# Padded operand tiles and rearranged joints in a two-block fp32 transformer kernel

## The chip, the cores and the metric

The kernel runs on one core of a Trainium2 chip. The metric is the device time of one launch in microseconds (us): before the change the median of three runs is 3501.79 us (3500.44 to 3502.34). The engines are named as in the profile: PE is TensorE (the matmuls), PEld its weight loads, DVE is VectorE, ACT is ScalarE, POOL is GpSimd, SP is the engine that issues most DMAs. SBUF is the on-chip memory, PSUM the accumulators of PE.

## The reference

256 tokens of width 2048 go through two blocks, all in fp32.

Block 1 normalises x, projects it by `w_in`, and feeds an RWKV-7 recurrence and a sparse causal attention; `w_mix_out` joins them. A cross-attention over 256 memory rows follows (`w_q_cross`, `w_kv_cross`, `w_o_cross`), then an MLP, `square(relu(rms_norm(h) @ w_up)) @ w_down` with 8192 hidden columns, and a final norm.

Block 2 puts 16 meta tokens in front, projects by `w_in_2`, runs 8 stick-breaking heads and 8 forgetting heads, joins them by `w_out_2`, and ends in an expert layer:

```
q = h @ w_query;  s = q . sub_keys;  top 16 of each half, top 16 of their sums
idx, g = the 16 experts of each of 8 heads, softmax of their scores
a = gelu(u[idx] . h);   out = sum over h,k of (g * a) * v[idx]
```

There are 16384 experts with a row of 2048 in `u` and one in `v`.

## The kernel before

**The matmuls.** Tokens lie along the free dimension: a tile holds 128 features on the partitions and 256 tokens beside each other. A product of 2048 features is 16 such tiles. Every fp32 operand is split into a high part and a low part of a shorter format (`xh`, `xl` for tokens; `whi`, `wlo` for weights), and each block of 128x128 weights takes three matmuls, high by high, high by low, low by high, which add up in one PSUM tile `plin`. A column of 128 outputs over 2048 features is 48 matmuls. The token operand is the one that streams through PE (the moving operand, 256 columns); the 128x128 weights are loaded first.

**The weights.** `half` (L285) loads 512 KB of weights, eight 128x128 blocks, into one of four `raw` buffers through SP's queue. ACT copies each 128x512 quarter of it to `whi`, DVE subtracts to get `wlo`. `linear` (L305) walks the columns and asks for a half whenever eight blocks are used up; each finished column goes to an `evac` function, by which DVE (and ACT, POOL) take it out of PSUM.

**The norms.** A norm's factor per token needs a sum of squares over all features: POOL or ACT square and add, `colsum` sums over partitions by four small matmuls (`pcs`), DVE takes an inverse square root in a chain of small operations on 128x2 elements (`rsv`, `rsh`, `rst`, `ldr`), and `bcast` spreads it over the partitions by matmuls (`pbc`). The factor is applied after the projection. For x, `load_norm` (L425) calls `inv_rms` (L458) right after the loads. In the cross-attention's output, `out` (L1219) adds a column to `h`, splits it and has POOL square and add it (`sqt`, `acc`), column by column; its first four columns are computed together, in four PSUM tiles.

**The expert layer.** All of `u` is multiplied (`pu`, 256 halves, tokens `ph`/`pl` moving), so that `A` holds gelu(u . h) for all 16384 experts and 256 tokens; `et` is the product times the norm's factor, on its way to `A`. The chosen g are scattered by indirect DMAs (`gd`) into a table in DRAM, which is zero elsewhere. `experts_out` (L1753) then takes the experts in 128 groups j: it loads the group's g (128x256, behind a dependency on the complete table), POOL multiplies it by `A`, ACT and DVE split it into `wh` and `wl`, and two halves of `pv` are multiplied with it into eight PSUM tiles `o`. Here the roles are changed: `wh` and `wl` are the loaded 128x128 operand, and the weights `whi` and `wlo` are the moving one, 512 columns at a time.

**Order and places.** The order on each engine is worked out when the program is built, from the order of the code, from a simulation of durations, and from marks: `high_priority` lifts what is in it forward, `keep_in_program_order` (in `half`: `pin`) holds a DMA at its place among the other pinned ones. Tiles of a pool are laid out one behind the other in the order in which they are first asked for, at multiples of 32 bytes within each partition. So a tile that is asked for and never used moves those behind it.

Of the kernel before, what the change touches and what calls it, by code (L numbers as in the profile page):

```python
# [8 lines left out]
F32 = mybir.dt.float32  # L9
# [3 lines left out]
AF = mybir.ActivationFunctionType  # L13
OP = mybir.AluOpType
# [3 lines left out]
S = 256  # L18
D = 2048
KT = D // 128  # L20
NMETA = 16
# [100 lines left out]
NCOL_IN = len(W_COLS)  # L122
# [61 lines left out]
def _layout(inp):  # L184
    a = {k: np.asarray(v) for k, v in inp.items()}
    o = {}
    o["x"] = _tT(a["x"][0])
    o["mem"] = _tT(a["mem"][0])
    o["pos"] = np.ascontiguousarray(a["positions"].reshape(1, S))
    o["vecs"] = _vecs(a)  # L190
    cc = _const_arrays()
    o["ident"] = np.ascontiguousarray(cc["ident"])
    o["iota"] = np.ascontiguousarray(cc["iota"])
    o["consts_a"] = np.ascontiguousarray(np.concatenate([cc[n] for n in CA], 1))
    o["dups"] = np.ascontiguousarray(np.concatenate([cc["dup"], cc["rdup"]], 1)[:64])
# [12 lines left out]
    fl = np.concatenate([w2[:, 7168:], w2[:, 7168:], np.zeros((D, 112), w2.dtype)], 1)  # L208
    qkv = w2[:, :6144].reshape(D, 2, 3, 8, 128).transpose(0, 1, 3, 2, 4).reshape(D, 6144)
    o["w_in2"] = _blocks(np.concatenate([qkv[:, :3072], fl, qkv[:, 3072:], w2[:, 6144:7168]], 1))  # L210
    o["w_out2"] = _blocks(a["w_out_2"][0])
    o["w_pq"] = _blocks(a["peer_w_query_2"][0])
    o["keys"] = np.ascontiguousarray(a["peer_sub_keys_2"][0].reshape(16, NKEY, 128).transpose(2, 0, 1))
    u = a["peer_u_2"][0].reshape(NKEY, NKEY, KT, 128)
    o["pu"] = np.ascontiguousarray(
        u.transpose(1, 3, 2, 0).reshape(NKEY, 128, 2, 8, 128).transpose(0, 2, 1, 3, 4)).reshape(2 * NKEY, 128, 8, 128)
    v = a["peer_v_2"][0].reshape(NKEY, NKEY, 2, 1024)
    o["pv"] = np.ascontiguousarray(v.transpose(1, 2, 0, 3)).reshape(2 * NKEY, 128, 8, 128)
    return o
# [25 lines left out]
class Kernel:  # L245
# [180 lines left out]
    def load_norm(self, src, gain, xh, xl, dst, eps, acc, w, tiles):  # L426

        nc = self.nc
        ts = []
        for q in range(4):  # L430
            t = tiles(q)
            with self.tc.high_priority():
                self.tc.keep_in_program_order(nc.sync.dma_start(t, src[:, 4 * q:4 * q + 4]))
            ts.append(t)
            if q < 2:
                self.ahead.append(self.half(w[len(self.ahead)], True))
            for k in range(4):
                self.split(xh[:, 4 * q + k], xl[:, 4 * q + k], t[:, k], self.v(gain, 4 * q + k))
            if q:
                self.squares(ts[q - 1], acc, q == 1, q == 1)  # L440
        with self.tc.high_priority():
            self.tc.keep_in_program_order(nc.sync.dma_start(self.ident, self.io["ident"]))
        self.squares(ts[3], acc, False)
        self.inv_rms(dst, acc, eps)

    def squares(self, t, acc, first, pool=False):

# [9 lines left out]

    def inv_rms(self, dst, acc, eps):  # L458
        r = self.small("ldr")
        with self.tc.high_priority():  # L460
            p = self.colsum([acc[:, 0], acc[:, 1]], S)
            self.rsqrt(r, p[:, 0:2], 1.0 / D, eps)
            self.bcast(dst, r, S)

    def block1(self, c0):
        nc, tc = self.nc, self.tc
# [4 lines left out]
        xp = self.pool("xa", 1, xstack)  # L471
        yp = self.pool("yp", 1, xstack)
        ctx = ExitStack()
        cp = self.pool("ca", 1, ctx)
        ph = self.pool("pa", 1, ctx)
        ca = cp.tile([128, wid], F32, name="ca")
        C = {n: ca[:, o:o + w] for n, (o, w) in off.items()}
        self.C = C
        xh = xp.tile([128, KT, S], F32R, name="xh", tag="xh")
        xl = xp.tile([128, KT, S], F32R, name="xl", tag="xl")  # L480
        rx = ph.tile([128, S], F32, name="rx")
# [63 lines left out]

        def evac(c, p):
            kind, g, q = KIND[c]
            if kind == "dsa":
                self.dsa_evac(g, p)
            elif kind == "rwkv":  # L550
                w, j = divmod(q, 2)
# [6 lines left out]
                shift(c, p, cur["AR"][:, j, 1] if w == 0 else cur["KV"[w - 1]][:, j])  # L558
                if q == 5:
                    rs.append(self.rwkv_group(g, cur["AR"], cur["K"], cur["V"], fr))  # L560
            elif g == 0:
                self.first = shift(c, p, L)
                self.act(th, L[0:64], AF.Tanh)
                ds.append(loads())
                ds.append(low_rank())
                ds.append(self.tables())
            elif g == 1:
                shift(c, p, M)
                self.act(sM[64:96], M[64:96], AF.Sigmoid)
                ds.append(self.dsa_ki())  # L570
            else:
                shift(c, p, XG)
                self.act(XG, XG, AF.Sigmoid)
# [8 lines left out]
        self.ds = (ds, ds2)  # L582

        def dense():
            yield from self.linear(self.io["w_in"], 0, NCOL_IN, KT, xh, xl, S, evac, more=(2,))
            rm = ph.tile([128, S], F32, name="rm")
            kv = self.kv = kvp.tile([128, 8, S], F32, name="kv", tag="kv")

# [16 lines left out]
                    self.squares(tile(c), xacc, c == 0)  # L605

            yield from self.linear(self.io["w_kvc"], 0, 8, KT, xh, xl, S, kv_evac)
            self.inv_rms(rm, xacc, 1e-5)
            for c in range(8):
                self.gtt(kv[:, c], kv[:, c], rm, OP.mult)  # L610

# [506 lines left out]
            self.gtt(acc, acc, t, OP.add)  # L1118

    def rstd(self, acc, dst, eps, dim=D):  # L1120
        p = self.colsum([acc], S)
        r = self.small("rr")
        self.rsqrt(r, p[:, 0:2], 1.0 / dim, eps)
        self.bcast(dst, r, S)
        return r
# [39 lines left out]
    def cross(self, cp, cxh, cxl, rc):  # L1165
# [48 lines left out]

        self.drive(self.linear(self.io["w_qc"], 0, 4, KT, cxh, cxl, S, query), todo, 1, flush=False)
        self.mxh, self.mxl = self.pair(self.xb)
        acc = wk.tile([128, S], F32, name="acc2", tag="acc", bufs=2)

        def out(c, p):  # L1219
            self.vtt(h[:, c], p, h[:, c], OP.add)  # L1220
            self.norm_tile(c, h[:, c], "norm_mlp", self.mxh[:, c, 0:S], self.mxl[:, c, 0:S], acc, wk)


        first = [self.plin.tile([128, 512], F32, name="plin", tag="plin") for _ in range(2)] + [self.ps("pc"), self.ps("pc")]
# [23 lines left out]
            out(c, first[c][:, 0:S])  # L1248
        self.lin(self.io["w_oc"], 2, KT - 4, 4, oh, ol, S, out, c0=4)
        self.rm = wk.tile([128, S], F32, name="rmlp", tag="rc", bufs=2)  # L1250
        self.rstd(acc, self.rm, 1e-5)

    def mlp(self, up):
        nc, h, wk = self.nc, self.h, self.wk
        U = {}
        g12 = wk.tile([128, KT], F32, name="g12")
        o1, o2 = self.vec["norm_final"][0], self.vec["norm_mix_2"][0]
        self.vtt(g12, self.vecs[:, o1:o1 + KT], self.vecs[:, o2:o2 + KT], OP.mult)
# [51 lines left out]
            if g < 3:  # L1310
                up_cols(g + 1, 1, 15)

        p1, p2 = self.colsum([acc1], S), self.colsum([acc2], S)
        r1, m, r2 = self.small("r1"), self.small("m2"), self.small("r2")
        self.rsqrt(r1, p1[:, 0:2], 1.0 / D, 1e-5)
        self.vtt(m, r1, r1, OP.mult)
        self.vtt(m, m, p2[:, 0:2], OP.mult)
        self.rsqrt(r2, m, 1.0 / D, 1e-6)
        self.vtt(r2, r2, r1, OP.mult)
        self.bcast(self.r12[:, NMETA:], r2, S)  # L1320
        r1b = wk.tile([128, S], F32, name="r1b", tag="rc", bufs=2)
        self.bcast(r1b, r1, S)
        for c in range(KT):
            self.gtt(h[:, c], h[:, c], r1b, OP.mult)

    def meta_tokens(self):

# [20 lines left out]
    def block2(self):  # L1348
# [8 lines left out]
        nc.sync.dma_start(ca, self.io["consts_b"])  # L1357
        C = self.C = {n: ca[:, o:o + w] for n, (o, w) in off.items()}
        bxh, bxl, r12 = self.bxh, self.bxl, self.r12
        rs = wk.tile([128, S], F32, name="r12s", tag="rc", bufs=2)  # L1360
        self.ts(rs, r12[:, NMETA:], 128 ** -0.5, None, OP.mult)
        gq = self.small("gq", 1)
        self.ts(gq, self.v("fox_q_gain_2", 0), 128 ** -0.5, None, OP.mult)

# [3 lines left out]
        yh, yl = self.pair(self.pool("xxb", 1, mx, side="right"))  # L1368
        acc_sb = wk.tile([128, S], F32, name="accsb", tag="acc", bufs=2)
        acc_fo = wk.tile([128, S], F32, name="accfo", tag="acc", bufs=2)  # L1370
        s0, s1 = [], []
        NB = [(0, 128), (128, 128), (256, 16)]
        X16 = b2.tile([16, SP], F32, name="X16")
        B16 = b2.tile([16, SP], F32, name="B16")
# [154 lines left out]
        def evac(c, p):  # L1529
            if c == 24:  # L1530
                forget(p)
            elif c < 49:
                hd, w = divmod(c - (c > 24), 3)
                nn, n0 = ((S, NMETA), (SP, 0), (SP, 0))[w]
                t = cur[w] = b2.tile([128, nn], F32, name="qkv"[w] + "_", tag="qkv"[w], bufs=3)
                self.vtt(t, p, rs if c < 24 and w == 0 else r12[:, n0:], OP.mult)
                if w == 2:
                    st = (s0, s1)[hd % 2]
                    st.append((stick if hd < 8 else fox)(hd % 8, cur[0], cur[1], t))
# [21 lines left out]
            self.vtt(h[:, c], p, h[:, c], OP.add)  # L1561
            self.norm_tile(c, h[:, c], "norm_ffn_2", self.pxh[:, c, 0:S], self.pxl[:, c, 0:S], acc, wk)

        self.lin(self.io["w_out2"], 0, KT, KT, yh, yl, S, out)
        self.rf = self.xa.tile([128, S], F32, name="rf")
        self.rstd(acc, self.rf, 1e-6)
        mx.close()
# [192 lines left out]
    def experts_out(self, es):  # L1760
        nc, A, sp = self.nc, self.A, self.sp
        with ExitStack() as c:
# [12 lines left out]
            for j in range(NKEY):  # L1775
                w = A[j // 32][:, j % 32]
                with self.tc.high_priority():
# [4 lines left out]
                        self.tc.add_manual_dep(i.ins, x.ins.name, order if prev else sync, reason="the table is complete")  # L1782
                    prev = i
                    self.gtt(g, w, g, OP.mult)
                    wh, wl = ((sp if j == 0 else vp).tile([128, S], F32R, name=n) for n in ("wh", "wl"))
                    self.split(wh, wl, g)
                for hf in range(2):
                    hi, lo = self.half(self.io["pv"][2 * j + hf])
                    first, last = j == 0, j == NKEY - 1
                    for d in range(2):  # L1790
                        for b in range(2):
# [31 lines left out]
```

## Time and profile before

| | |
|---|---|
| median of 3 runs | 3501.79 us (3500.44 to 3502.34) |
| the profiled execution | 3498.64 us |
| its span, first to last instruction | 3496.9 us |
| PE busy | 3451.6 us, 99% of the span |
| PEld, DVE, ACT, POOL busy | 93%, 66%, 50%, 25% |
| mean granted clock of PE | 0.996 |

The span is 1.7 us shorter than the profiled execution's own time. Matmuls overlap: one lasts some 0.28 us from its start to its modelled end, and the next starts 0.12 us after it. What a matmul costs is therefore read from starts, or from the number of matmuls in a stretch in which PE is always busy, and not from the mean duration in a group. A granted clock of 1.00 is PE's higher level (2.4 GHz), 0.50 its lower one (1.2 GHz).

### The profile page before, as it was taken

The page shows a single profiled execution, that of the slowest core. Times are in us where ns is not written, and L with a number is a line of the kernel's source. Part 1 is how long each engine was busy: PE and PEld are TensorE (multiplying, and loading weights), DVE is VectorE, ACT ScalarE, POOL GpSimd, SP SyncE. Part 2 cuts the span into 40 slices and gives each one's busy share as a digit, 9 for nine tenths or more (in the row PEclk, how much of TensorE's full clock was granted, in tenths as well). Part 3 has the DMA queues.
Part 4 walks back from the last instruction along what each step waited for, and adds up shares of the span by engine and source line. Part 5 has one row for each costly group of instructions (what it writes and reads, how often), then busy time and mean ns, then how long its engine had stood idle before and what let it go on. Part 6 is the DMA issues. An engine that isn't in the chain of part 4 may idle for free.

```text
span 3496.9 us, 72405 instructions
## 1 busy us (share of the span) xinstructions
PE 3451.6 (99%) x28376; PEld 3240.5 (93%) x28376; DVE 2298.9 (66%) x4248; ACT 1762.9 (50%) x3187; POOL 880.1 (25%) x788
## 2 busy tenths in 40 slices
PE   8999999999999999999999999999999999999999
PEld 7899889899999999999999999999999888888887
DVE  7678767765656568656557799755555566666666
ACT  5444555554545455444445455555555455555554
POOL 2222213310101015200003002777777011111111
PEclk9999999999999999999999999999999999999999
DMA  5333435476767575544345656777777666666666
GB/s 198 113 119 128 165 124 184 148 218 192 226 190 228 185 230 183 158 145 145 121 133 176 202 180 188 185 186 186 187 187 185 206 210 213 211 213 211 210 214 194
DMA packets 230279, 635.99 MB, mean 182 GB/s; under 512 B 58320, under 2 KB 75408, under 8 KB 229552
## 3 DMA queue, kind: packets, MB, share of 16 engines
q1 hardware_dynamic: 193072, 631.22, 57.5%
q0 software_dynamic: 36864, 0.15, 2.3%
q8 instruction: 222, 3.64, 0.4%
q14 instruction: 121, 0.99, 0.1%
HBM read 610.16 MB, written 21.10 MB: 181 GB/s over the span
## 4 chain that ended last, share of the span: by engine, by line
PE 96%; DVE 2%; DMA 1%; issue 1%; ACT 0%; POOL 0%; DVEq 0%; SPq 0%; ACTq 0%; POOLq 0%
PE plin L255 68%; PE o L255 21%; PE po L255 1%; DVE wlo L261 1%; PE pfz L255 1%; PE pw L255 0%; PE pbc L255 0%; DMA hd<-ht 0%; PE pz L255 0%; PE pix L255 0%; PE pcs L255 0%; PE px L751 0%; PE pt L751 0%; DVE xl L264 0%; PE py L255 0%
## 5 line engine op out<-in xcount | busy, mean ns | idle before, releaser
L261 DVE TENSOR_TENSOR wlo<-raw,whi 128x512 fp32r<-128x512 f32 x2208 | 1602.7, 728 | 959.2 <-ACT whi L276 857.9
L276 ACT ACTIVATE whi<-raw 128x512 fp32r<-128x512 f32 x2208 | 1388.7, 630 | 1445.4 <-PE plin L255 988.5
L255 PE MATMUL plin<-ph,wlo 128*128 128x256 f32 (+1 forms) x4560 | 1290.8, 283 | 2.2 <-DVE wlo L261 2.2
L255 PE MATMUL plin<-pl,whi 128*128 128x256 f32 (+1 forms) x4560 | 1291.0, 283 | 0.0
L255 PE MATMUL plin<-ph,whi 128*128 128x256 f32 (+1 forms) x4560 | 1285.1, 282 | 1.6 <-DVE ut L261 0.7
L255 PEld LDWEIGHTS plin<-ph,wlo 128*128 128x128 f32 x4560 | 863.7, 190 | 4.5 <-DVE wlo L261 2.4
L255 PEld LDWEIGHTS plin<-ph,whi 128*128 128x128 f32 x4560 | 863.4, 189 | 3.0 <-issue 1.6
L255 PEld LDWEIGHTS plin<-pl,whi 128*128 128x128 f32 x4560 | 858.4, 188 | 1.6 <-issue 1.1
L1668 POOL DMA_INDIRECT gd<-GT,EI x256 | 414.7, 1620 | 347.5 <-DMA raw<-in_pu_dram 218.8
L255 PE MATMUL o<-wlo,wh 128*128 128x512 f32 x1024 | 405.8, 396 | 0.0
L255 PE MATMUL o<-whi,wl 128*128 128x512 f32 x1024 | 404.4, 396 | 0.0
L255 PE MATMUL plin<-xh,whi 128*128 128x256 f32 x1136 | 327.9, 289 | 9.0 <-ACT whi L276 8.4
L255 PE MATMUL plin<-xh,wlo 128*128 128x256 f32 x1136 | 327.4, 289 | 4.1 <-DVE wlo L261 3.9
L255 PE MATMUL plin<-xl,whi 128*128 128x256 f32 x1136 | 326.9, 288 | 1.7 <-DVE xl L264 1.7
L255 PE MATMUL o<-whi,wh 128*128 128x512 f32 x1024 | 323.4, 397 | 3.9 <-ACT wh L276 3.9
L255 PE MATMUL plin<-uh,wlo 128*128 128x256 f32 x1024 | 289.7, 283 | 0.0
L255 PE MATMUL plin<-ul,whi 128*128 128x256 f32 x1024 | 289.7, 283 | 0.0
L255 PE MATMUL plin<-uh,whi 128*128 128x256 f32 x1024 | 289.6, 283 | 0.0
L258 POOL TENSOR_TENSOR g<-A,g 128x256 f32<-128x256 f32 x128 | 105.8, 827 | 668.0 <-DMA g<-gd 546.1
L255 PEld LDWEIGHTS o<-whi,wh 128*128 128x128 f32 x1024 | 193.3, 189 | 50.9 <-ACT wh L276 4.1
L255 PEld LDWEIGHTS o<-wlo,wh 128*128 128x128 f32 x1024 | 193.4, 189 | 46.1
L255 PEld LDWEIGHTS o<-whi,wl 128*128 128x128 f32 x1024 | 192.2, 188 | 47.2
(563 smaller groups left out, 3520.4 us busy)
## 6 DMA issues: line engine op xcount, KB each, us to landing
raw<-in_pu_dram SPq DMA_DIRECT2D x256, 512.0 KB
raw<-in_pv_dram SPq DMA_DIRECT2D x256, 512.0 KB
raw<-in_w_in_dram SPq DMA_DIRECT2D x208, 512.0 KB
raw<-in_w_up_dram SPq DMA_DIRECT2D x128, 512.0 KB
raw<-in_w_down_dram SPq DMA_DIRECT2D x128, 512.0 KB
raw<-in_w_mix_dram SPq DMA_DIRECT2D x32, 512.0 KB
gd<-zero SPq DMA_DIRECT2D x64, 256.0 KB
raw<-in_w_out_dram SPq DMA_DIRECT2D x32, 512.0 KB
```

The lines of the kernel that those rows point to most:

```text
L255: self.nc.tensor.matmul(out, l, r, start=start, stop=stop)
L258: self.nc.gpsimd.tensor_tensor(out, a, b, op=op)
L261: return self.nc.vector.tensor_tensor(out, a, b, op=op)
L276: return self.nc.scalar.activation(out, a, AF.Copy, **kw)
L1668: i = self.nc.gpsimd.indirect_dma_start(self.gd, bass.IndirectOffsetOnAxis(self.EI[tb][:, s:s + 1], 0), self.GT[tb][:, s:s + 1], None, com ...
```

## The change

There are two kinds of edits. **Pads:** three tiles that nothing uses move the tiles behind them in their pool. The byte addresses within a partition in the built programs are:

| tiles | pad | before | after | remainder by 256 |
|---|---|---|---|---|
| `xh`, `xl` | 32 bytes | 60256, 76640 | 60288, 76672 | 96 to 128 |
| `uh` (two buffers) | 96 bytes | 54112, 70496 | 54208, 70592 | 96 to 192 |
| `ul` (two buffers) | the same | 86880, 103264 | 86976, 103360 | 96 to 192 |
| `wh` (two buffers, j > 0) | 480 bytes | 192896, 193920 | 193376, 194400 | 128 to 96 |
| `wl` (two buffers, j > 0) | the same | 194944, 195968 | 195424, 196448 | 128 to 96 |
| `whi` (four buffers) | none | 35680 and on, by 2048 | the same | 96 |
| `wlo` (four buffers) | none | 43872 and on, by 2048 | the same | 96 |

In `xh`, `xl`, `uh` and `ul` the 16 slices are 1024 bytes apart, so that all of a tile have one remainder; in `ph` and `pl` (unchanged, of 272 tokens) they are 1088 bytes apart and take the remainders 32, 96, 160 and 224 in turn.

**Joints** are the places between two products. J1: x's `inv_rms` is called in `evac` after column 2, and the first three columns are taken out of PSUM behind it. J2: for the memory rows the priority mark stands at the call. J3: in the cross-attention's output the squares are taken by ACT, four columns at once, and POOL adds them. J4: the MLP's tail is a generator that block 2 steps through. J5: the first four columns of `w_out_2` are computed together in four PSUM tiles, the features in the outer loop, and its layout in DRAM follows. J6: in `experts_out` the loads of group 0 are pinned.

```diff
@@ load_norm, inv_rms
         self.squares(ts[3], acc, False)
-        self.inv_rms(dst, acc, eps)
...
         r = self.small("ldr")
-        with self.tc.high_priority():
-            p = self.colsum([acc[:, 0], acc[:, 1]], S)
...
+        p = self.colsum([acc[:, 0], acc[:, 1]], S)
@@ block1
+        xp.tile([128, 8], F32, name="xpad")
         xh = xp.tile([128, KT, S], F32R, name="xh", tag="xh")
...
+            if c < 3:
+                early.append((c, p))
+                if c == 2:
+                    self.inv_rms(rx, xacc, 1e-5)
+                    for e in early:
+                        lead(*e)
...
-            yield from self.linear(self.io["w_in"], 0, NCOL_IN, KT, xh, xl, S, evac, more=(2,))
+            yield from self.linear(self.io["w_in"], 0, NCOL_IN, KT, xh, xl, S, evac, more=(2, 3))
@@ cross-attention, out
-            self.norm_tile(c, h[:, c], "norm_mlp", self.mxh[:, c, 0:S], self.mxl[:, c, 0:S], acc, wk)
+            self.split(self.mxh[:, c, 0:S], self.mxl[:, c, 0:S], h[:, c], self.v("norm_mlp", c))
+            if c % 4 == 3:
+                t = cp.tile([128, 4, S], F32, name="hsq", tag="hsq", bufs=2)
+                self.act(t, h[:, c - 3:c + 1], AF.Square)
+                if c == 3:
+                    self.gtt(acc, t[:, 0:2], t[:, 2:4], OP.add)
+                else:
+                    self.gtt(t[:, 0:2], t[:, 0:2], t[:, 2:4], OP.add)
+                    self.gtt(acc, acc, t[:, 0:2], OP.add)
@@ mlp
+        up.tile([128, 24], F32, name="upad")
...
+        def tail():
+            p1, p2 = self.colsum([acc1], S), self.colsum([acc2], S)
...
@@ block2, w_out_2
-        self.lin(self.io["w_out2"], 0, KT, KT, yh, yl, S, out)
+        p = [self.plin.tile([128, 512], F32, name="plin", tag="plin") for _ in range(2)] + [self.ps("pc"), self.ps("pc")]
+        for k in range(KT):
+            if k % 2 == 0:
+                w = self.half(self.io["w_out2"][k // 2])
+            for c in range(4):
...
+        for c in range(4):
+            out(c, p[c][:, 0:S])
+        self.lin(self.io["w_out2"], 8, KT - 4, KT, yh, yl, S, out, c0=4)
@@ experts_out
+                    if j == 0:
+                        vp.tile([128, 120], F32, name="vpad", bufs=1)
...
-                    hi, lo = self.half(self.io["pv"][2 * j + hf])
+                    hi, lo = self.half(self.io["pv"][2 * j + hf], j == 0)
```

At x's norm, DVE's program stands as follows before and after (`wlo` are the low parts of weights, the rest is the chain of the inverse square root).

```order
L261 TENSOR_TENSOR wlo<-raw,whi 128x512 x2
L270 TENSOR_SCALAR rsv<-pcs 128x2
L268 TENSOR_SCALAR rsh<-rsv 128x2
L270 TENSOR_SCALAR ldr<-rsh 128x2
L261 TENSOR_TENSOR rst<-ldr 128x2
L261 TENSOR_TENSOR wlo<-raw,whi 128x512
L264 SCALAR_TENSOR_TENSOR rst<-rst,rsv 128x2
L261 TENSOR_TENSOR wlo<-raw,whi 128x512
L264 SCALAR_TENSOR_TENSOR ldr<-rst,ldr 128x2
```

```order
L262 TENSOR_TENSOR wlo<-raw,whi 128x512 x8
L271 TENSOR_SCALAR rsv<-pcs 128x2
L269 TENSOR_SCALAR rsh<-rsv 128x2
L271 TENSOR_SCALAR ldr<-rsh 128x2
L262 TENSOR_TENSOR rst<-ldr 128x2
L265 SCALAR_TENSOR_TENSOR rst<-rst,rsv 128x2
L265 SCALAR_TENSOR_TENSOR ldr<-rst,ldr 128x2
```

The two `wlo` stand ahead of the chain instead of inside it, and the chain comes one column of matmuls later; on PE `pcs` and `pbc` stand next to each other both times.

On POOL, at the cross-attention's output, there were 31 operations of 128x256 on `sqt` and `acc` (the first ones are shown), and there are seven of 128x512 (all are shown).

```order
L258 TENSOR_TENSOR acc_9108<-h 128x256
L258 TENSOR_TENSOR sqt<-h 128x256 x2
L258 TENSOR_TENSOR acc_9108<-acc_9108,sqt 128x256 x2
L258 TENSOR_TENSOR sqt<-h 128x256
L258 TENSOR_TENSOR acc_9108<-acc_9108,sqt 128x256
```

```order
L259 TENSOR_TENSOR acc_9109<-hsq 128x512
L259 TENSOR_TENSOR hsq<-hsq 128x512
L259 TENSOR_TENSOR acc_9109<-acc_9109,hsq 128x512
L259 TENSOR_TENSOR hsq<-hsq 128x512
L259 TENSOR_TENSOR acc_9109<-acc_9109,hsq 128x512
L259 TENSOR_TENSOR hsq<-hsq 128x512
L259 TENSOR_TENSOR acc_9109<-acc_9109,hsq 128x512
```

The squaring has gone to ACT (four `hsq<-h` of 128x1024), and POOL begins only after the fourth column.

On SP, where the expert layer's second product begins, `g<-gd` is the load of a group's g and `in_pv` a half of its weights.

```order
L289 DMA raw<-in_pu_dram 128x1024 x256
L289 DMA raw<-in_pv_dram 128x1024 x5
L1779 DMA g<-gd 128x256 x3
L289 DMA raw<-in_pv_dram 128x1024
L1796 DMA res<-hd 128x2x2048
```

```order
L290 DMA raw<-in_pu_dram 128x1024 x256
L1819 DMA g<-gd 128x256
L290 DMA raw<-in_pv_dram 128x1024 x2
L1819 DMA g<-gd 128x256
L290 DMA raw<-in_pv_dram 128x1024 x2
L1819 DMA g<-gd 128x256
L1838 DMA res<-hd 128x2x2048
```

The first g has moved ahead of all of `pv`, from behind five halves that each wait for a free `raw` buffer. On ACT the split `wh` of group 0 now stands right behind the last `A`, and before the first `whi` of `pv`.

## Rows read from the trace of the kernel before

**Rows 1.** The page's busy line and its chain by line.

```profile
PE 3451.6 (99%) x28376; PEld 3240.5 (93%) x28376; DVE 2298.9 (66%) x4248; ACT 1762.9 (50%) x3187; POOL 880.1 (25%) x788
...
PE plin L255 68%; PE o L255 21%; PE po L255 1%; DVE wlo L261 1%; PE pfz L255 1%; PE pw L255 0%; PE pbc L255 0%; DMA hd<-ht 0%; PE pz L255 0%; PE pix L255 0%; PE pcs L255 0%; PE px L751 0%; PE pt L751 0%; DVE xl L264 0%; PE py L255 0%
```

**Rows 2.** The waits of PE (total us, times, longest us).

```profile
PE plin L255 <- DVE wlo L261: 6.1, 5, 2.2
PE plin L255 <- DVE h L261: 4.2, 7, 2.6
PE o L255 <- ACT wh L276: 3.9, 1, 3.9
PE pbc L255 <- DVE ldr L264: 3.4, 1, 3.4
```

**Rows 3.** Four stretches: length, PE busy (matmuls), granted clock, DMA share, GB/s.

```profile
540.00:600.00 60.00, 60.00 (x503) 1.00 0.58 187
800.00:860.00 60.00, 60.00 (x502) 1.00 0.59 187
2100.00:2700.00 600.00, 600.00 (x5073) 1.00 0.74 186
2790.00:3490.00 700.00, 700.00 (x3001) 1.00 0.66 209
```

**Rows 4.** Groups of PE by line and shape, their counts and busy times.

```profile
L255 PE MATMUL plin<-xh,whi 128*128 128x256 f32 x1136 | 327.9, 289 | 9.0 <-ACT whi L276 8.4 <-ACT xh L276 0.5
L255 PE MATMUL plin<-uh,whi 128*128 128x256 f32 x1024 | 289.6, 283 | 0.0
L255 PE MATMUL o<-whi,wl 128*128 128x512 f32 x1024 | 404.4, 396 | 0.0
```

**Rows 5.** DVE in order of time near 28 us (start, duration, instruction).

```profile
28.13 0.16 DVE L261 TENSOR_TENSOR rst<-ldr 128x2 f32<-128x2 f32 x1
28.21 0.69 DVE L261 TENSOR_TENSOR wlo<-raw,whi 128x512 fp32r<-128x512 f32 x1
28.82 0.15 DVE L264 SCALAR_TENSOR_TENSOR rst<-rst,rsv 128x2 f32<-128x2 f32 x1
```

**Rows 6.** Four more stretches of PE, columns as in the other stretches.

```profile
30.30:33.70 3.40, 2.83 (x13) 0.50 0.46 154
651.50:654.90 3.40, 3.40 (x19) 0.50 0.30 118
1842.80:1846.20 3.40, 3.25 (x15) 0.50 0.35 96
2771.20:2778.00 6.80, 5.08 (x12) 0.50 0.98 379
```

**Rows 7.** DVE in order of time near 650 us.

```profile
648.71 1.21 DVE L261 TENSOR_TENSOR wlo<-raw,whi 128x512 fp32r<-128x512 f32 x1
649.84 0.83 DVE L264 SCALAR_TENSOR_TENSOR pl<-h,vecs,ph 128x256 fp32r<-128x256 f32 x1
650.59 0.41 DVE L261 TENSOR_TENSOR h<-plin,h 128x256 f32<-128x256 f32 x1
652.54 0.67 DVE L261 TENSOR_TENSOR wlo<-raw,whi 128x512 fp32r<-128x512 f32 x1
```

**Rows 8.** The chain that ended last, near 2770 us.

```profile
2768.21 3.24 DMA g<-gd
2771.70 0.73 POOL g L258
2772.45 0.42 ACT wh L276
```

**Rows 9.** SP's queue in order of time, from 2754 us.

```profile
2756.22 11.69 SPq L289 DMA_DIRECT2D raw<-in_pv_dram  x5
```

**Rows 10.** ACT in order of time near 2769 us.

```profile
2768.97 0.63 ACT L276 ACTIVATE whi<-raw 128x512 fp32r<-128x512 f32 x1 [0.74 <-DVE wlo L261]
2769.55 0.42 ACT L273 ACTIVATE A<-et 128x256 f32<-128x256 f32 x1
```

More of the change, by code (lines that the diff above doesn't have):

```diff
@@ L210, in _layout @@
     o["w_in2"] = _blocks(np.concatenate([qkv[:, :3072], fl, qkv[:, 3072:], w2[:, 6144:7168]], 1))
-    o["w_out2"] = _blocks(a["w_out_2"][0])
+    o["w_out2"] = np.concatenate([_blocks(a["w_out_2"][0][:, :512].reshape(KT, 128, 4, 128).transpose(0, 2, 1, 3)
+                                          .reshape(KT * 4 * 128, 128)), _blocks(a["w_out_2"][0][:, 512:])])
     o["w_pq"] = _blocks(a["peer_w_query_2"][0])
@@ L459, in inv_rms @@
         r = self.small("ldr")
-        with self.tc.high_priority():
-            p = self.colsum([acc[:, 0], acc[:, 1]], S)
-            self.rsqrt(r, p[:, 0:2], 1.0 / D, eps)
-            self.bcast(dst, r, S)
+        p = self.colsum([acc[:, 0], acc[:, 1]], S)
+        self.rsqrt(r, p[:, 0:2], 1.0 / D, eps)
+        self.bcast(dst, r, S)
     def block1(self, c0):
@@ L547, in evac @@
             kind, g, q = KIND[c]
-            if kind == "dsa":
+            if c < 3:
[4 more added lines that the diff above has]
+                        lead(*e)
+            elif kind == "dsa":
                 self.dsa_evac(g, p)
@@ L560, in evac, with lead @@
                     rs.append(self.rwkv_group(g, cur["AR"], cur["K"], cur["V"], fr))
-            elif g == 0:
+        early = []
+        def lead(g, p):
+            c = g
+            if g == 0:
                 self.first = shift(c, p, L)
@@ L607, in dense @@
             yield from self.linear(self.io["w_kvc"], 0, 8, KT, xh, xl, S, kv_evac)
-            self.inv_rms(rm, xacc, 1e-5)
+            with tc.high_priority():
+                self.inv_rms(rm, xacc, 1e-5)
             for c in range(8):
@@ L1120, in rstd @@
     def rstd(self, acc, dst, eps, dim=D):
-        p = self.colsum([acc], S)
+        p = self.colsum(acc if isinstance(acc, list) else [acc], S)
         r = self.small("rr")
@@ L1216, in cross @@
         self.mxh, self.mxl = self.pair(self.xb)
-        acc = wk.tile([128, S], F32, name="acc2", tag="acc", bufs=2)
+        acc = wk.tile([128, 2, S], F32, name="acc2", tag="acc2")
         def out(c, p):
             self.vtt(h[:, c], p, h[:, c], OP.add)
-            self.norm_tile(c, h[:, c], "norm_mlp", self.mxh[:, c, 0:S], self.mxl[:, c, 0:S], acc, wk)
+            self.split(self.mxh[:, c, 0:S], self.mxl[:, c, 0:S], h[:, c], self.v("norm_mlp", c))
[7 more added lines that the diff above has]
+                    self.gtt(acc, acc, t[:, 0:2], OP.add)
         first = [self.plin.tile([128, 512], F32, name="plin", tag="plin") for _ in range(2)] + [self.ps("pc"), self.ps("pc")]
@@ L1250, in cross @@
         self.rm = wk.tile([128, S], F32, name="rmlp", tag="rc", bufs=2)
-        self.rstd(acc, self.rm, 1e-5)
+        self.rstd([acc[:, 0], acc[:, 1]], self.rm, 1e-5)
     def mlp(self, up):
@@ L1311, in mlp @@
                 up_cols(g + 1, 1, 15)
[L1313 to L1324, printed above, removed]
+        def tail():
+            p1, p2 = self.colsum([acc1], S), self.colsum([acc2], S)
+            r1, m, r2 = self.small("r1"), self.small("m2"), self.small("r2")
+            self.rsqrt(r1, p1[:, 0:2], 1.0 / D, 1e-5)
+            self.vtt(m, r1, r1, OP.mult)
+            self.vtt(m, m, p2[:, 0:2], OP.mult)
+            self.rsqrt(r2, m, 1.0 / D, 1e-6)
+            self.vtt(r2, r2, r1, OP.mult)
+            yield
+            self.bcast(self.r12[:, NMETA:], r2, S)
+            self.rs = wk.tile([128, S], F32, name="r12s", tag="rc", bufs=2)
+            self.ts(self.rs, self.r12[:, NMETA:], 128 ** -0.5, None, OP.mult)
+            r1b = wk.tile([128, S], F32, name="r1b", tag="rc", bufs=2)
+            self.bcast(r1b, r1, S)
+            for c in range(KT):
+                self.gtt(h[:, c], h[:, c], r1b, OP.mult)
+        self.tail = tail()
     def meta_tokens(self):
@@ L1359, in block2 @@
         bxh, bxl, r12 = self.bxh, self.bxl, self.r12
-        rs = wk.tile([128, S], F32, name="r12s", tag="rc", bufs=2)
-        self.ts(rs, r12[:, NMETA:], 128 ** -0.5, None, OP.mult)
         gq = self.small("gq", 1)
@@ L1370, in block2 @@
         acc_fo = wk.tile([128, S], F32, name="accfo", tag="acc", bufs=2)
-        s0, s1 = [], []
+        s0, s1 = [self.tail], []
         NB = [(0, 128), (128, 128), (256, 16)]
@@ L1535, in evac @@
                 t = cur[w] = b2.tile([128, nn], F32, name="qkv"[w] + "_", tag="qkv"[w], bufs=3)
-                self.vtt(t, p, rs if c < 24 and w == 0 else r12[:, n0:], OP.mult)
+                self.vtt(t, p, self.rs if c < 24 and w == 0 else r12[:, n0:], OP.mult)
                 if w == 2:
@@ L1562, in out @@
             self.norm_tile(c, h[:, c], "norm_ffn_2", self.pxh[:, c, 0:S], self.pxl[:, c, 0:S], acc, wk)
-        self.lin(self.io["w_out2"], 0, KT, KT, yh, yl, S, out)
+        p = [self.plin.tile([128, 512], F32, name="plin", tag="plin") for _ in range(2)] + [self.ps("pc"), self.ps("pc")]
[3 more added lines that the diff above has]
+            for c in range(4):
+                hi, lo = (self.block(x, 4 * (k % 2) + c) for x in w)
+                o = p[c][:, 0:S]
+                self.mm(o, hi, yh[:, k, 0:S], k == 0, False)
+                self.mm(o, hi, yl[:, k, 0:S], False, False)
+                self.mm(o, lo, yh[:, k, 0:S], False, k == KT - 1)
+        for c in range(4):
+            out(c, p[c][:, 0:S])
+        self.lin(self.io["w_out2"], 8, KT - 4, KT, yh, yl, S, out, c0=4)
         self.rf = self.xa.tile([128, S], F32, name="rf")
```

## The prediction

> **What bounds the kernel now.** I read the page first: PE is busy for 99% of the span, and its two kinds of product, `plin` and `o`, carry 89% of the chain that ended last [rows 1]. So a microsecond counts only if it goes from PE: either a place where PE stands still, or the time that one matmul takes. The waits of PE come next [rows 2]. The long ones among them are the places that the joints touch: 3.4 us at x's norm, 2.6 of 4.2 us in the cross-attention's output, 3.9 us at the start of the expert layer's second product. Then the stretches in which PE never stops, to see what one matmul costs [rows 3]. A stretch counts the two or three matmuls that reach in over its edge; without them, 60 us hold 500 matmuls on `xh`/`xl` (from 540 us) and 500 on `uh`/`ul` (from 800 us), 120.0 ns each. On `ph`/`pl` (from 2100 us) 600 us hold some 5071, 118.3 ns each; on `o`, with 512 columns (from 2790 us), 700 us hold 3000, 233.3 ns each. Last, the stretches after the long waits: PE was granted 0.50 of its clock there, 1.2 GHz [rows 6].
>
> **The pads.** They change no instruction; they move operands. Every slice of `xh`, `xl`, `uh` and `ul` goes from one remainder (96 by 256) to another (128 or 192). Counts: three groups of 1136 on `xh`/`xl` are 3408 matmuls, three of 1024 on `uh`/`ul` are 3072, together 6480; `o` has three of 1024, 3072 [rows 4]. That an address can matter is what rows 3 show: `ph` and `uh` do the same work with the same weights' tiles, and differ in where the token slices lie (remainders in turn against one alone), and the one takes 118.3 and the other 120.0 ns. No row shows a token tile at remainder 128 or 192, so I bound it from both sides. Below: 256 further columns cost 233.3 - 120.0 = 113.3 ns, so a matmul has a fixed part of 6.7 ns, and if a better place removed it all, the gain would be 6480 x 6.7 = 43.4 us. Above: `ph`'s mean covers places above and below it, so a place may be as much worse than 120.0 as 118.3 is better, 1.7 ns, +11.0 us. I take the nearest row, 118.3: **-11.0 us** (6480 x 1.7). Almost all these matmuls stand in stretches that PE bounds, so the gain is not hidden; but a faster PE needs `whi` and `wlo` earlier, and DVE, 66% busy, has the room.
>
> `wh` and `wl` move to remainder 96, that of `whi` and `wlo`, which stream through PE there. They are the loaded operand; no row shows that its place matters: **0**. Bounds: `uh` against `whi`, both at 96, is the slow pair of the two, 1.7 ns in 256 columns, so 3.4 in 512; 3072 x 3.4 = 10.4 us, either way.
>
> **The joints.** J1: the chain on DVE has two `wlo` inside; a step that follows without one takes 0.20 us, and here 28.82 - 28.13 = 0.69 [rows 5]. Twice 0.49 is 1.0 us off the wait of 3.4. The chain now stands behind `wlo` x8, whose halves PE needs soon anyway, and `pw`, `pa` and what follows the tokens' shift come a column later, beside PE's own work. The remaining 2.4 us still lower the clock, as now [rows 2, 6]. I take **-0.7**, between +0.5 (the chain waits for a `wlo` whose half has not landed) and -2.4 (the clock stays up; its stretch holds some nine matmuls).
>
> J2 and J4: PE's order is unchanged there, and DVE's only by a copy: **0**, ±0.5.
>
> J3: the wait of 2.6 us ends with DVE's `h`, behind work that runs beside POOL: a `wlo` takes 1.21 us there and 0.67 once POOL is idle, a `pl` 0.83, while the `h` alone took 0.41 [rows 7]. Now POOL begins only after the fourth column, so two `wlo` lose 0.54 each and two `pl` some 0.4 each: 1.9 us. PE then waits 0.7 us and should keep its clock: the stretch from 651.50 us holds 16 matmuls after its edge is taken off, in 3.40 us instead of 1.92, so 1.5 more [rows 6]. The other six waits sum to 1.6 us [rows 2]; POOL still works beside DVE, with seven larger operations instead of 31, and I halve them: 0.8. Sum **-4.2** (-1.5 if the clock falls all the same and later waits stay; -5.7 if all goes). What is late next is the sum of squares: after the last column ACT squares 1024 elements and POOL adds twice, but the first use of the factor lies a whole column of 48 matmuls, 5.8 us, behind. The four squares on ACT stand beside a queue that is idle half the time [rows 1]; without that cover they would delay `whi`, at most what is halved above.
>
> J5: four columns now end together, and the fifth finds no free PSUM tile until DVE has added `h` for the first (0.41 us), perhaps behind a `wlo` (0.67) [rows 7]. Before, one tile came free while the other filled. **+0.7** (0 to +1.3). The 2.2 us of `wlo` stand before this product, in `w_in_2`, and stay [rows 2, 6].
>
> J6: the load of the first g was issued at 2768.21 us, behind five halves of `pv` that took SP 11.69 us from 2756.22 on, waiting for buffers [rows 8, 9]. It took 3.24 us, then POOL 0.73, `wh` 0.42, and PE began at 2772.9. Now g and its product are ready before 2760, and group 0 waits for ACT: the last `A` begins at 2769.55 and takes 0.42 [rows 10], then `wh` 0.42, then the first `whi` 0.63 (which used to be done before), with the steps between them some 0.05: 2771.1. That is 1.8 us earlier. The wait left is 3.9 - 1.8 = 2.1 us, just under the shortest after which the clock fell, 2.2 [rows 2, 6]. If it holds, the 12 matmuls of the stretch from 2771.20 take 2.80 instead of 5.08 us, 2.3 less. I take half of that: **-3.0** (-1.8 to -4.1).
>
> **Sum.** -0.7 - 4.2 + 0.7 - 3.0 = -7.2 for the joints, -11.0 for the pads, -18.2. On the profiled execution's 3498.64 us that is 3480.4. That execution lies 3.15 us below the median; on the median, 3483.6.
>
> **A rule against the pads.** In rows 3 the same 256 columns take 120.0 and 118.3 ns. The Trainium skill, "SBUF — State Buffer", Specifications, says that SBUF is read in lines of 16 bytes and that each new line costs. All places here are multiples of 32, so by that rule the number of lines is the same before and after, and the pads give nothing. Rows 3 are against it, since `ph` and `uh` begin at line borders too; it is rival B below. The skill's page "TensorE: Matmul & The Clock Gate" (section "Wait — 56ns, not 53.3ns?") gives a matmul in a row its columns over 2.4 GHz and about 2.5 ns; for 256 columns that would be an estimated 109.2 ns. No row here comes so low, and by it the pads' gain would be at most 6480 x 10.8 = 70 us, beyond my range.
>
> **Rivals.**
> A. The whole fixed part goes for the padded tiles. For it: rows 3 put 6.7 ns into every matmul whatever its columns, and the tiles' remainder by 64 changes from 32 to 0, which none of the tiles that stream through PE has now. Against: `ph` visits four remainders and its mean moves by only 1.7. It gives -43.4 - 7.2 = -50.6: 3451.
>
> B. The places have no effect, or that of `xh`/`uh` (-11.0) is given back by `wh`/`wl` (+10.4). For it: `o` has the lowest time for a column of all rows, and its two operands differ in remainder now and agree afterwards. Only the joints are left: 3494.6, with their own bounds 3491 to 3500.
>
> C. Slower: the new remainder is a worse one. `ph`'s mean hides places on both sides of 118.3, and the pads choose 128 and 192, which no row shows. At +1.7 ns for 6480 matmuls (+11.0) and +3.4 for `o` (+10.4), less 7.2 for the joints, it is +14.2: 3516. It decides from a rise of 1.1 ns (7.2 over 6480) on; against it is that 120.0 is the slowest of the rows of 256 columns already.
>
> **How the numbers follow.** Chances: the forecast 0.45, A 0.25, B 0.18, C 0.12. The forecast's own range is 3474 to 3491. A change below 0.2%, 7 us, can't be told from none in this kernel. Faster than 3494.8 are the forecast, A and not quite half of B: 0.45 + 0.25 + 0.08 = 0.78. The rest of B, 0.10, and a little of C (the joints beside a small loss), 0.02, are the same: 0.12. Slower: 0.10. The range goes from A's middle, 3449, to B's upper end, 3502; it leaves out C and the gains beyond A.
>
> **What would show it.** In the profile after: the matmuls on `xh` and `uh` 118.3 ns from start to start (113.3 by A, 120.0 by B, 121.7 by C), and `o` at 233.3 (236.7 where B or C's second half holds); `ph` unchanged at 118.3. The wait of `pbc` 2.4 us, the longest of `plin` on `h` under 1 us with the clock up behind it, that of `o` on ACT 2.1 us, and one of some 0.7 us in the fifth column of `w_out_2`. The forecast is wrong where the first two stay at 120.0, or fall by a multiple of 1.7.

## The result, and the profile after

The changed kernel takes 3463.25 us (median of 4 runs, 3460.29 to 3468.21) against 3502.07 (3500.44 to 3502.41): ratio 0.9891, 95% interval 0.9874 to 0.9909, or 38.8 us less. The forecast was 3483.6, 18 us less. The profiled execution took 3460.29 us.

The page's busy line of the kernel after. PE is still the bound:

```profile
PE 3414.5 (99%) x28380; PEld 3224.0 (93%) x28380; DVE 2291.8 (66%) x4248; ACT 1766.1 (51%) x3191; POOL 864.6 (25%) x764
```

The stretches of the kernel after in which PE never stops, columns as in [rows 3] (length, PE busy and matmuls, granted clock, DMA share, GB/s):

```profile
540.00:600.00 60.00, 60.00 (x516) 1.00 0.59 189
800.00:860.00 60.00, 60.00 (x504) 1.00 0.61 197
2100.00:2700.00 600.00, 600.00 (x5073) 1.00 0.74 186
2790.00:3440.00 650.00, 650.00 (x2869) 1.00 0.68 218
```

This is where most of the time went. With the two or three matmuls at the edges taken off, as in the prediction, `xh` has gone from 120.0 to about 117 ns, `uh` has stayed at 120.0, `ph`, which was not touched, at 118.3, and `o` has gone from 233.3 to 226.7. The largest step is on the product whose pad the prediction priced at nothing: 3072 x 6.6 = 20.3 us.

The waits of PE after, as in [rows 2]:

```profile
PE plin L256 <- DVE wlo L262: 8.2, 9, 1.8
PE plin L256 <- DVE h L262: 3.5, 6, 1.3
PE pbc L256 <- DVE ldr L265: 2.8, 1, 2.8
PE o L256 <- ACT whi L277: 1.8, 1, 1.8
```

The long waits at the joints are shorter; those on `wlo` have grown from 6.1 to 8.2 us in sum. In three places where the clock was at 0.50 before [rows 6], this execution kept it: after the cross-attention's output begins, after the wait on `wlo` in `w_in_2` (which is no joint), and at the start of `o`. The columns are those of [rows 3]; the granted clock, behind the count of matmuls, is 1.00 in all three:

```profile
640.00:644.00 4.00, 2.87 (x22) 1.00 0.65 242
1829.00:1833.00 4.00, 2.56 (x21) 1.00 0.13 38
2756.50:2760.50 4.00, 3.94 (x17) 1.00 0.85 336
```

From the starts of the matmuls the time can be put down to stages: x's projections 595.9 to 587.8 us, the cross-attention's output (its first matmul to its last) 36.6 to 32.5, from the MLP's end to the first `o` 1365.1 to 1361.2, and `o` 719.0 to 696.4. The rest moved by 0.4 us together; within it, the step from the cross-attention's last matmul to the MLP's first grew from 0.6 to 1.5 us.

### The profile page after: what moved, and what is told of

It is laid out like the page before. It is cut to its first block, busy times and chain, and to the rows that moved or that the text cites. A ratio compares the mean times of both kernels' runs of the same rounds, so it can differ in the third digit from the quotient of the medians.

```text
span 3458.1 us, 72390 instructions
## 1 busy us (share of the span) xinstructions
PE 3414.5 (99%) x28380; PEld 3224.0 (93%) x28380; DVE 2291.8 (66%) x4248; ACT 1766.1 (51%) x3191; POOL 864.6 (25%) x764
## 5 line engine op out<-in xcount | busy, mean ns | idle before, releaser
L256 PE MATMUL o<-wlo,wh 128*128 128x512 f32 x1024 | 398.7, 389 | 0.0
L256 PE MATMUL o<-whi,wh 128*128 128x512 f32 x1024 | 314.9, 389 | 1.8 <-ACT whi L277 1.8
```

Source lines behind the costliest of these rows:

```text
L256: self.nc.tensor.matmul(out, l, r, start=start, stop=stop)
```

## The experiments

**One part at a time.** Is it the pads by themselves, or the order at the joints?

First the pad ahead of `wh` and `wl` alone:

```diff
+                    if j == 0:
+                        vp.tile([128, 120], F32, name="vpad", bufs=1)
                     wh, wl = ((sp if j == 0 else vp).tile([128, S], F32R, name=n) for n in ("wh", "wl"))
```

> The kernel before with the 480 bytes ahead of wh and wl alone. Theory P (the pads act by themselves, and the one ahead of the loaded operand, priced at nothing in the prediction, is the large one): o goes from 233.3 to 226.7 ns, everything else stays; 3072 x 6.6 = 20 us, so about 3482 us. Rival J (the expert layer is faster because its start was rearranged, and the pad is idle): o stays at 233.3 ns and the time at 3502 us.

Measured: 3479.19 us, ratio 0.9941 (0.9925 to 0.9958). The stretch on `o` of this kernel, in which 670 us hold some 2956 matmuls, 226.7 ns each:

```profile
2790.00:3460.00 670.00, 670.00 (x2958) 1.00 0.70 217
```

One unused tile of 480 bytes is worth 20.4 us. Rival J is out.

Then the pads of the tokens' tiles alone:

```diff
+        xp.tile([128, 8], F32, name="xpad")
...
+        up.tile([128, 24], F32, name="upad")
```

> The kernel before with the 32 bytes ahead of xh and xl and the 96 bytes ahead of uh and ul, nothing else. Theory P: xh 120.0 to 117 ns, uh stays at 120.0 in the mean, o 233.3; 3408 x 2.9 = 10 us, so about 3492 us. Rival J (block 1 gains by the norm's later place): xh stays at 120.0 and the time at 3502 us.

Measured: 3493.87 us, 0.9982 (0.9972 to 0.9992), 5.8 us less, with an interval that reaches to 9.8. Its stretches on `xh`, `uh` and `o`:

```profile
540.00:600.00 60.00, 60.00 (x517) 1.00 0.61 189
800.00:860.00 60.00, 60.00 (x503) 1.00 0.63 193
2790.00:3460.00 670.00, 670.00 (x2873) 1.00 0.67 212
```

`xh` takes 117 ns without any joint; `uh` gains nothing by its 96 bytes. The gain in time is smaller than the 10 us expected. In the trace the short matmuls on `xh` fell as expected, but what else belongs to the stage of x's projections took some 4 us longer than before, 1.4 of them a wait of PE on the norm's sum (`xacc`) that the trace before does not have. Whether the pads or this one execution made that wait was not tried.

And the joints alone, the changed kernel with its three pads taken out:

> The changed kernel without its three pads. Theory P: xh and uh 120.0, o 233.3 ns; only the joints are left, worth 7 to 9 us by the stretches of the two traces: about 3494 us. Rival J: xh 117 and o 226.7 ns here too, about 3464 us.

Measured: 3491.68 us, 0.9977 (0.9967 to 0.9988), 8.0 us less. Its stretches on the same three:

```profile
540.00:600.00 60.00, 60.00 (x502) 1.00 0.56 183
800.00:860.00 60.00, 60.00 (x502) 1.00 0.64 193
2790.00:3460.00 670.00, 670.00 (x2874) 1.00 0.67 212
```

All three are back at 120.0, 120.0 and 233.3. The parts sum to 34.2 us of 38.8, within their intervals.

**Which place counts?** A first map, with rotating places for several operands at once:

```diff
-                h, l = (p.tile([128, QB, 128], F32R, name=n, tag=n) for p, n in ((self.phi, "whi"), (self.plo, "wlo")))
+                h = self.phi.tile([128, QB * 128 + 8], F32R, name="whi", tag="whi")[:, 0:QB * 128].rearrange("p (a b) -> p a b", b=128)
+                l = self.plo.tile([128, QB, 128], F32R, name="wlo", tag="wlo")
...
+        self.plo.tile([128, 32], F32, name="lpad", bufs=1)
...
+                    wh, wl = (sp.tile([128, S], F32R, name=n) if j == 0 else vp.tile([128, S + 8], F32R, name=n, bufs=8)[:, 0:S] for n in ("wh", "wl"))
```

> The changed kernel with places that rotate: the four buffers of whi at remainders 96, 128, 160 and 192 by 256 (2080 bytes apart), those of wh and wl, eight each, at all multiples of 32; wlo stays at 96, xh at 128, uh at 192. In o every pair of (streaming whi, loaded wh or wl) comes up some hundred times. Theory T1 (the two places against each other): the time of a matmul follows the difference, 226.7 ns where both agree and 233.3 where they are 32 apart, whatever whi's own place. Theory T2 (the loaded operand's own place): 226.7 for wh at 32, 96, 160, 224 and 233.3 for 0, 64, 128, 192, whatever whi's. Theory T3 (the streaming operand's own place): the time changes with whi's remainder and not with that of wh. In block 1 whi is the loaded operand: by T1 and T2 the time on xh goes in steps with the buffer.

Measured: inconclusive for all three theories. The mean on `o` was 231.9 ns; with `whi` at 96 and `wh` at 96 a matmul took 232.1, not 226.7, and with both at 160, 230.8. By the starts in the trace, a matmul's time spread by 3.20 ns. Grouped by three addresses (its own streaming operand, the next loaded one, the next streaming one), each by 256, the spread left is 2.42; by 512, 2.08; by 1024, 0.74 (200 groups of some 15 matmuls, their number allowed for). So the time is set by places, but by those of the neighbours too, and a map in which they all change cannot show a pair's own worth: here `wl` and `wlo` stood elsewhere than `wh` and `whi`.

The second map keeps the neighbours alike. d is the streaming operand's place less the loaded one's:

```diff
+                        wh, wl = (vp.tile([128, 2 * S], F32R, name=n)[:, 8 * (j % 16):8 * (j % 16) + S] for n in ("wh", "wl"))
...
+        xx = xp.tile([128, 2 * KT * S + 32], F32R, name="xh", tag="xh")
+        xh, xl = (Places(xx, lo, (4, 3, 3, 3, 3), 8) for lo in (0, 1))
```

(`Places` hands out the 16 slices of high and low parts in groups, each group 32 bytes further on; `uh`/`ul` likewise.)

> The changed kernel with whi and wlo where they are (remainder 352 by 512) and the other operand of each product put at many places, 32 bytes apart: wh and wl of group j, both alike, 32 x (j mod 16) further on; the slices of xh/xl in five groups at 64 to 192 bytes from whi's remainder by 512, those of uh/ul at 224 to 352 in one buffer and 384 to 512 in the other. d is the streaming operand's place less the loaded one's by 512. Theory D (the difference by 512 decides): o takes 226.7 ns at d = 0 and 233.3 at d = -32, as in the kernels after and before; xh and uh take 120.0 at d = 0 and 96 and 117 at d = 32; and what is above columns / 2.4 GHz (13.3, 20.0, 10.3 ns so far) is one function of d for 256 and 512 columns. Rival R (the loaded operand's own place decides): with whi loaded at one place the times on xh and uh do not change with d, apart from where a group begins. Rival M (no order in it that a difference explains): at d = 0 and d = 96 the times are others than 120.0, because the neighbours' places changed.

Measured, from the starts in the trace (means over triples whose successor has the same d; for `o` over the six matmuls of a `whi` and its `wlo`, d by 256):

```
256 columns   d   64    96   128   160   192   224   256   288   320   352   384   416   448   480   512=0
             ns  117.8 119.4 118.5 117.6 115.6 118.2 118.3 118.8 118.6 118.3 119.0 118.6 115.0 117.6 119.7
512 columns   d    0    32    64    96   128   160   192   224
             ns  227.0 233.1 229.4 233.5 233.3 233.7 233.4 233.0
```

D holds in that each width has its curve of d, and that the known points come back (d = 0 and 96 near 120, and 226.7 to 227.0 on `o`). R falls, since the times on `xh` and `uh` change while `whi` stays, and so does M. What fell of D is the last clause: the curves are not one. With 512 columns agreement is the best place; with 256 columns it is among the worst (119.7, beside 119.4 at d = 96), and the best is 64 bytes before a multiple of 256. The map for 256 columns is coarse: where the counting begins at the second or third matmul of a triple instead of the first, its means move by up to 1.7 ns, most at d = 448. It shows which places are short, not their exact times, and it cannot tell d from d + 256.

**The crossing test.** If the difference decides, `whi` can go to `wh` as well as `wh` to `whi`:

```diff
         self.phi = self.pool("whi", PARTS)
+        self.phi.tile([128, 8], F32, name="hpad", bufs=1)
...
+                    if j == 0:
+                        vp.tile([128, 56], F32, name="vpad", bufs=1)
```

> The kernel before with 32 bytes ahead of whi, which move whi, wlo, xh, xl, uh and ul alike to remainder 128 by 256, and with wh and wl held at their own remainder of before, 128. So in o the streaming operand has moved to the loaded one, where the change had moved the loaded one to the streaming one; on xh and uh both have moved and d stays 0. Theory D (the difference decides): o 226.7 ns, xh and uh 120.0 as before; 20 us below before. Rival L (wh and wl are better off at 96 than at 128): o stays at 233.3. Rival S (xh is better off at 128 than at 96, as in the changed kernel): xh goes to 117.

Measured: 3485.31 us in one run, beside 3502.17. The stretches on `xh`, `uh`, `ph` and `o`:

```profile
540.00:600.00 60.00, 60.00 (x503) 1.00 0.60 191
800.00:860.00 60.00, 60.00 (x503) 1.00 0.62 186
2100.00:2700.00 600.00, 600.00 (x5050) 1.00 0.75 185
2790.00:3460.00 670.00, 670.00 (x2957) 1.00 0.70 218
```

`o` takes 226.7 with `wh` at its old place, and `xh`, now at 128 as in the changed kernel but with `whi` moved along, is at 120.0. L and S are out: neither of these operands has a good place of its own. The run gained 16.9 us instead of 20. `ph`, which stayed where it was while `whi` moved, is the likely reason: its stretch holds 5050 matmuls where the kernel before had 5073, 118.9 ns each instead of 118.3. This product was in no theory's forecast, and it too changed by the other operand's place.

**All products at good places.** The changed kernel with d = 448 for `uh`/`ul` and those `ph`/`pl` that hold 256 tokens, 192 for `xh`/`xl`, 0 for `o`:

```diff
-        xp.tile([128, 8], F32, name="xpad")
+        xp.tile([128, 48], F32, name="xpad")
...
+        return tuple(pool.tile([128, KT * SP], F32R, name=n, tag=n)[:, at:at + KT * S].rearrange("p (k s) -> p k s", s=S)
+                     for n in ("ph", "pl"))
...
-        up.tile([128, 24], F32, name="upad")
+        up.tile([128, 112], F32, name="upad")
```

> The changed kernel with the places that the map of pairs showed to be the shortest for 256 columns, each kept over a whole tile: uh/ul at d = 448 (448 bytes of pad instead of 96), xh/xl at 192 (192 instead of 32), and those ph/pl that need only 256 tokens with slices 1024 instead of 1088 bytes apart, at d = 448; wh/wl stay at d = 0. Theory D (a pair's difference sets the time of each matmul): uh 115.0, ph 115.0, xh 115.6 ns; 3072 x 5.0 + 10944 x 3.3 + 3408 x 1.3 = 56 us below the changed kernel's 3463, about 3407 us. Rival N (the short times in the map came from neighbours at other places): these tiles come out at 117 to 120 ns, about 3450 us or more.

Measured: 3389.9 us (3387.53 to 3412.69), ratio to before 0.9703 (0.9666 to 0.9740). Its stretches on `xh`, `uh`, `ph` and `o`:

```profile
540.00:600.00 60.00, 60.00 (x532) 1.00 0.66 197
780.00:860.00 80.00, 80.00 (x708) 1.00 0.72 209
2080.00:2580.00 500.00, 500.00 (x4414) 1.00 0.81 195
2770.00:3370.00 600.00, 600.00 (x2649) 1.00 0.72 218
```

`uh` and `ph` take 113.3 ns in these stretches, with no spread beyond the trace's steps of 1 ns, and `xh` 113 to 115. That beats the kernel before by 111 us and the changed one by 73, more than the 56 expected: the map's groups had shown 115.0, and a place kept over a whole tile comes out shorter. N is out.

> The same with d = 192 for uh/ul and those ph/pl as well. Theory D with a period of 256 bytes, as o showed it: d = 192 and 448 are the same place, uh, ph and xh all at 115.0 to 115.6 ns, and the time that of the run at 448 within some 5 us. Rival: the period is 512, and the two runs differ by more than 1 ns in a matmul, 14 us or more.

Measured: 3401.89 us, 0.9736 (0.9691 to 0.9780), the median of 3385, 3388, 3416 and 3419; why they lie apart is not known. So the times of the two kernels cannot settle it: the medians differ by 12 us, more than the 5 expected, and the ranges overlap. The traces can. The stretches on `uh` and `ph`, beside 708 and 4414 matmuls in the kernel at d = 448:

```profile
780.00:860.00 80.00, 80.00 (x708) 1.00 0.72 210
2080.00:2580.00 500.00, 500.00 (x4414) 1.00 0.81 195
```

Both take 113.3 ns again. With 256 columns, too, these two places 256 bytes apart are the same; for other pairs of d and d + 256 no run shows it.

**Is there a shorter place for `o`?** In the kernel with all products at good places (d = 448), `wh` in steps of 16 bytes and `wl` in steps of 32, at all pairs of places:

```diff
+                        wh, wl = (vp.tile([128, 2 * S], F32R, name=n)[:, o:o + S] for n, o in (("wh", 4 * (j % 16)), ("wl", 8 * (j // 16))))
```

> The kernel with all places chosen, but wh of group j at 16 x (j mod 16) bytes from a start and wl at 32 x (j div 16), so that the two loaded operands of o stand at all pairs of places, wh in steps of 16 bytes. Theory D: the three matmuls of a triple take 226.7 ns where both agree with whi, some 229 to 231 where one does, and up to 235 elsewhere; steps of 16 bytes lie between their neighbours. Rival F (the shorter fixed part of 6.7 ns that uh and ph reached, 220.0 ns, is to be had in o too at a pair that the map of equal places didn't hold): some pair shows less than 226.

Measured, as above (a part of the table: d of `wh` down, d of `wl` across):

```
            0    32    64    96   128   160   192   224
   0     226.7 231.3 230.8 231.8 231.5 230.1 232.1 231.1
  16     226.7 231.2 228.8 229.9 232.0 229.9 233.3 232.1
  32     233.1 233.2 231.9 232.4 232.5 232.1 233.2 233.9
 240     226.7 232.2 232.4 232.0 231.7 232.8 232.9 232.8
```

No pair is under 226.7, and it takes both loaded operands: where only one of them is at d = 0, the whole table has 230.1 to 233.9, somewhat more than D's 229 to 231. A step of 16 bytes did not lie between its neighbours: with `wh` at 16 or 240 it is as good as at 0. F is out for these places; those of `wlo` against `whi` were not tried.

## Why the prediction was wrong, point by point

**The bound** was read rightly: PE, and there the time of one matmul.

**The step that failed** is the term of `wh` and `wl`: "They are the loaded operand; no row shows that its place matters: 0", with bounds of 10.4 us. The pad alone measured -20.4 us, twice the bound: 226.7 ns instead of 233.3 on `o`. The rows did hold the hint. I compared `uh` with `ph` as one operand's places, and took o's 233.3 and uh's 120.0 as one law, columns and a fixed part of 6.7 ns. They were two different pairs: `uh` at d = 0, and `o` at d = -32. At 2.4 GHz 256 columns are 106.7 ns and 512 are 213.3; what is left over is 13.3 at d = 0 for `uh` before and for `o` after, and 20.0 for `o` before. The low end of the bound came from the slow pair in 256 columns, and d = 0 turned out to be the best in 512.

**The tokens' pads** were taken at -11.0 us, 1.7 ns for all 6480. It came to 2.9 ns for `xh` (8.9 us over the 3109 matmuls that follow each other undisturbed in both traces) and nothing for `uh`, where d = 96 costs what d = 0 does. The nearest row, the mean of `ph` over several d, says nothing of a single d; the map's curve runs from 115 to 120 and the two pads fell on different points of it. That the sum comes near the forecast is luck: one tile gained almost twice what was forecast for it, the other nothing.

**The joints** were forecast at -7.2 us and measured at -8.0, by misses that partly cancel. J3, forecast at -4.2, came to -4.1 between the first and the last matmul of the stage. As the prediction put it, DVE is quicker without POOL beside it: POOL begins only at 640.89, and a `wlo` takes 0.68 instead of 1.21 [rows 7]. The kernel after, POOL and then DVE:

```profile
640.89 1.29 POOL L259 TENSOR_TENSOR acc<-hsq 128x512 f32<-128x512 f32 x1 [42.51 <-ACT hsq L274]
```

```profile
639.68 0.68 DVE L262 TENSOR_TENSOR wlo<-raw,whi 128x512 fp32r<-128x512 f32 x1
640.28 0.47 DVE L265 SCALAR_TENSOR_TENSOR pl<-h,vecs,ph 128x256 fp32r<-128x256 f32 x1
```

A part of that came back right behind the stage, which the prediction had not reckoned with. Its later and larger sums on POOL run beside the last columns; a `wlo` takes 1.77 us there, and at the MLP's first matmul PE waits 1.25 us on the `h` behind it, where it waited 0.35 before. With this step J3 comes to -3.2. POOL, DVE and PE after:

```profile
657.15 1.34 POOL L259 TENSOR_TENSOR acc<-acc,hsq 128x512 f32<-128x512 f32 x1
```

```profile
657.28 1.77 DVE L262 TENSOR_TENSOR wlo<-raw,whi 128x512 fp32r<-128x512 f32 x1
658.97 0.41 DVE L262 TENSOR_TENSOR h<-plin,h 128x256 f32<-128x256 f32 x1
```

```profile
659.53 0.36 PE L256 MATMUL plin<-ph,whi 128*128 128x256 f32 x1 [1.25 <-DVE h L262]
```

J6 went the way it was drawn, and the better of the two halves: the wait is 1.8 us instead of 3.9, on `whi`, behind the last `A` and `wh`, and in this execution the clock stays up. ACT and then PE of the kernel after:

```profile
2755.27 0.42 ACT L274 ACTIVATE A<-et 128x256 f32<-128x256 f32 x1 [5.26 <-DVE et L262]
2755.59 0.40 ACT L277 ACTIVATE wh<-g 128x256 fp32r<-128x256 f32 x1
2755.90 2.18 ACT L277 ACTIVATE whi<-raw 128x512 fp32r<-128x512 f32 x4
```

```profile
2756.56 1.25 PE L256 MATMUL o<-whi,wh 128*128 128x512 f32 x4 [1.79 <-ACT whi L277]
```

J5 was wrong in a small thing. No wait came: the four columns do not end together but three matmuls apart, and DVE takes the first out before the fifth needs its tile. DVE and then PE after:

```profile
1854.76 0.42 DVE L262 TENSOR_TENSOR h<-plin,h 128x256 f32<-128x256 f32 x1 [0.54 <-PE plin L256]
```

```profile
1855.48 0.28 PE L256 MATMUL pc<-ph,wlo 128*128 128x256 f32 x1
1855.60 0.28 PE L256 MATMUL plin<-ph,whi 128*128 128x256 f32 x1
```

In J1 the chain's wait went from 3.4 to 2.8 us, 0.6 off where 1.0 was worked out. The wait on `wlo` in `w_in_2`, held to stay, went from 2.2 to 1.8 us; it was 1.7 with the joints alone and 2.2 with either set of pads alone, so it belongs to the joints, but why DVE is earlier there was not tried.

**The clock.** The prediction reckoned that the clock may hold behind a wait "just under the shortest after which the clock fell, 2.2". That was misread: in the kernel before it also fell at 685.7 us, with no wait over 0.7 us in the 8 us ahead. Nor did the shorter waits of the change keep it up by themselves. With the joints alone it fell in `w_in_2` behind 1.7 us, and in the kernel with all products at good places at the start of `o` behind the same 1.8 us on `whi`. The kernel before, that with the joints alone, and that at good places; the granted clock stands behind the count:

```profile
685.70:689.10 3.40, 3.40 (x19) 0.50 0.60 198
1837.90:1841.30 3.40, 3.40 (x18) 0.50 0.52 154
2686.50:2689.90 3.40, 3.40 (x10) 0.51 0.92 349
```

Of the seven traces of kernels with these joints, the clock held at the start of `o` in three. That the better half came was thus chance, as the prediction's half of 2.3 us allowed for; what decides it stays open.

**The rivals.** The measured 3463 us lies within the range and nearest to A's 3451, but by luck: A took it from `xh` and `uh`, and it came from `o`. (The range's lower end is called A's middle, 3449; A's own sum is 3451.) A's 6.7 ns exist, and `uh` and `ph` lost them in the run at d = 448, but not at the places of this change. B had the right thought, that the two operands of `o` would agree afterwards, with the wrong sign. The rule of the Trainium skill beside it ("SBUF — State Buffer", Specifications: SBUF is read in lines of 16 bytes) cannot explain the runs by itself: all places of the change are line borders, and `o` moved by 6.6 ns. The 109.2 ns, an estimate worked out from the Trainium skill, "TensorE: Matmul & The Clock Gate" (section "Wait — 56ns, not 53.3ns?"), were not reached; the lowest steady time in any run is 113.3.

## What to carry to other kernels

Where PE is the bound, compare the time between two starts with columns over the granted clock, for each product apart, and list the addresses of both operands beside it: what is left over may be the places of a pair. An unused tile of some bytes is then the cheapest experiment there is, but only with the other operand's address in view, and with places kept alike over a whole tile. Never bound the effect of one operand's place by a row in which both differ.

## What the runs showed of the hardware that was not expected

A matmul of 128x128 fp32 parts in a steady row took columns / 2.4 GHz (the granted clock was 1.00) and a rest that depended on d: with 256 columns 6.7 ns at d = 192 and 448, 10.3 at 32, 13.3 at 0 and, in the mean, at 96; with 512 columns, by 256, 13.3 at d = 0 and 16 to 20 elsewhere, where both loaded operands stood alike. At places that change from one matmul to the next its time followed three addresses by 1024 (the spread fell from 3.20 to 0.74 ns). Why the curve has this form, and why agreement is the best for one width and among the worst for the other, stays open.
